# Feed-forward weights of a two-layer trunk split in units of four blocks, and a fourth seven-product step in every second column group

## The chip, the cores and the metric

The kernel runs on one core of one Trainium2 chip. The metric is the device time of one execution, in microseconds. Beside the time there is a profile: one execution of the program taken by the hardware profiler, with each instruction's start, length and the event that released it.

## What is computed

The program is a trunk of two layers on 256 rows of width 2048, all in float32. Layer 0 mixes with sliding-window attention beside an mLSTM, layer 1 with forgetting attention. After either mixer comes a SwiGLU feed-forward part with hidden width 5632, and a last RMSNorm ends the trunk. The change touches the feed-forward part above all:

```python
def swiglu(xn, w_gate, w_up, w_down):
    return (jax.nn.silu(xn @ w_gate) * (xn @ w_up)) @ w_down
...
h = h + mix.astype(h.dtype)
h = h + swiglu(rms_norm(h, norm_ffn[layer]), w_gate[layer], w_up[layer], w_down[layer])
```

## The kernel before

**Three matmuls for one product.** A float32 operand is split into a rounded part `hi` and the rest `lo = x - hi`. A product is then the sum of three matmuls: left hi by right hi, left hi by right lo, left lo by right hi (`three`, L508 to L511; in the plain projections L212 to L214). Activations are split once. Every weight block of 128 rows by 512 columns is loaded from memory by a DMA on the queue of the sync engine SP (`load_raw`, L117), copied to `hi` on ScalarE (ACT) and subtracted to `lo` on VectorE (DVE) (`split_chunk`, L173 to L181). A load takes two blocks, one above the other (CK = 2): 128 partitions by 1024 elements, 512 KB. So the two lines L177 and L178 hold most of the ScalarE and VectorE work of the kernel.

**Column groups.** Gate and up have 11 groups of 512 columns per layer (`ffn`, L599). In one group `pair_group` (L516) walks over the 2048 rows of the weights as eight k pairs (256 rows each), with a list of steps such as

```python
ORDER = ((0, 0), (1, 1), (0, 2), (1, 3), (0, 4), (1, 5), (0, 6), (0, 7))
```

The second number is the k pair. A step with a leading 0 is a plain step: two row halves of the activations (t = 0, 1) by two k blocks by two matrices (gate and up, or two neighbouring column groups of down) are eight block products, 24 matmuls. A step with a leading 1 is a mixed step: seven block products give the same sums (Strassen's scheme in Winograd's form), so 21 matmuls, at the price of sums of blocks. On the side of the activations these sums are made once per pair (`sums_of`, L253, called where the pair's transposed activations come up) and kept in `sx` and `sd`. On the side of the weights VectorE makes four new blocks at every mixed step (L568 to L571), and the four are split again (`split_plain`, L338). Four of the seven products accumulate in banks of PSUM of their own (`prods`); after the last mixed step `combine` (L523 to L530) adds them up on VectorE into the tile `c`, and after the last plain step L619 adds the plain accumulators. SiLU (L621) and the product with up (L623) follow; the result is transposed by DMA (L646 to L648), joined and split a group later (`join`, L649).

The PSUM banks alternate: a group's plain accumulators sit in one pool of four banks, its `prods` in the other, and the next group has them the other way round (`bank`, L513). So a group's first plain products need the banks that `combine` of the group before has read out.

The eleven groups run in three parts (`PARTS`: 3, 4 and 4 groups). After a part follows its share of the down product, two runs of `pair_group` with 6 or 8 k pairs, of which 2 or 3 are mixed (`DOWN`).

**Buffers.** `hi` and `lo` of the weights come from a pool of six slots of two blocks (`wp`, L100), the raw blocks of plain steps from four slots of two (`wr`, L101), those of mixed steps from four slots of two in the layer's own pool (`RAWS`), and the four sums of a mixed step from two slots (`ht`, `lt`, L578). A slot is written again when the last reader of its old content is done; for `hi` and `lo` that is a matmul. In the mixers the same mixed step runs with other buffers (`halves` is given); there the change alters no amount of work.

**Order.** All instructions of an engine run in the order in which the program lists them. That list is made at build time by a planner that plays the program with its own costs; `run_due` (L188) and `issue_after` pin a few pieces of work to a step.

Of the kernel before, what the change touches and what calls it, by code (L numbers as in the profile page):

```python
# [17 lines left out]
P = 128  # L18
# [17 lines left out]
ORDER = ((0, 0), (1, 1), (0, 2), (1, 3), (0, 4), (1, 5), (0, 6), (0, 7))  # L36
# [15 lines left out]
RAWS = 4  # L52
# [20 lines left out]
def trunk(  # L73
# [26 lines left out]
    wp = ctx.enter_context(tc.tile_pool(name="wp", bufs=6))  # L100
    wr = ctx.enter_context(tc.tile_pool(name="wr", bufs=4))  # L101
# [15 lines left out]
    def load_raw(w, k0, c0, n, pool=wr, bufs=4, raws=None):  # L117
        if raws:
            raw = raws.pop(0)
            raws.append(raw)  # L120
        else:
            raw = pool.tile([P, CK, NB], F32, tag="raw", name="raw", bufs=bufs)
# [17 lines left out]
    first = wr.tile([P, CK, NB], F32, tag="raw", name="raw", bufs=4)  # L140
# [32 lines left out]
    def split_chunk(raw, n):  # L173
        hi = wp.tile([P, CK, NB], F32R, tag="hi", name="hi")
        lo = wp.tile([P, CK, NB], F32R, tag="lo", name="lo")
# [5 lines left out]
        return hi, lo  # L181

# [70 lines left out]
    def sums_of(pool, sh, sl, copies, full=None, tags=("tmp", "tmp"), bufs=None, box=None):  # L253
# [10 lines left out]
        nc.vector.tensor_tensor(out=s[:, 2, :], in0=full[:, 0, 0, :], in1=full[:, 0, 1, :], op=ALU.subtract)  # L264
# [62 lines left out]
    def scrap(fp, n):  # L327
# [3 lines left out]
        elif n == 3:  # L331
            halves = [fp.tile([P, 3, NB], F32, tag=f"sd{i}", name="box", bufs=1)[:, 0:CK, :] for i in range(2)]
        else:
            halves = [fp.tile([P, CK, NB], F32, tag="raw", name="box", bufs=RAWS) for _ in range(2)]
# [181 lines left out]
    def pair_group(fp, par, lhs, sums, mats, order, todo=(), halves=None, inner=None, raws=None):  # L516
# [6 lines left out]
        def combine(prods):  # L523
            c = fp.tile([P, 4, NB], F32, tag="c", name="c", bufs=1)
            nc.scalar.copy(c[:, 0, :], prods[0])
            nc.vector.tensor_tensor(out=c[:, 2, :], in0=prods[3], in1=c[:, 0, :], op=ALU.add)
# [5 lines left out]
        for pos, (kind, pair) in enumerate(order):  # L532
            k0 = 2 * pair
            if inner is not None and pos == len(order) - 1:
                c = combine(prods)
                inner()
            if not kind:
                last = pos == len(order) - 1
                walk = [(i, t) for i in range(CK) for t in range(NT)]
                if last:  # L540
                    walk.sort(key=lambda it: it[1])
                for m, (w, c0) in enumerate(mats):
                    hi, lo = load_chunk(w, k0, c0, NB)
                    run_due(todo, pos)
                    for i, t in walk:
# [3 lines left out]
                            plain[m][t], ah[:, ts], al[:, ts], hi[:, i, :], lo[:, i, :],  # L549
# [6 lines left out]
            ra, rb = (load_raw(w, k0, c0, NB, fp, W_RAWS if halves else RAWS, raws) for w, c0 in mats)  # L556
            hg, lg = split_chunk(ra, NB)
            run_due(todo, pos)
            t4 = ra if halves else fp.tile([P, 2, NB], F32, tag="t4", name="t4", bufs=1)
# [762 lines left out]
```

## Time and profile before

| | |
|---|---|
| runs | 2076.74, 2077.82, 2078.33 us; median 2077.82 us |
| span of the profiled execution | 2076.6 us (its own time is not listed beside it) |
| TensorE (PE) busy | 2066.4 us, 9473 matmuls |
| VectorE (DVE) busy | 1824.5 us, 2410 instructions |
| ScalarE (ACT) busy | 1374.7 us, 1736 instructions |
| read from memory | 408.68 MB |

A busy time is the sum of an engine's instruction spans with overlaps counted once. Matmul spans overlap each other, so the rate of TensorE is read from the distance of two starts, not from the length of one. In a view by stretches each row gives, for a stretch of the span, the busy time and number of instructions of each engine, the granted clock, the DMA share and GB/s. In a view in order of time a row gives start, length, engine, line, tiles and, in brackets, the idle time before it with what ended it.

### The profile page before, as it was taken

The numbers are of one execution on the slowest core, as the hardware profiler recorded it, in microseconds if no ns is written. First come the engines' busy times: TensorE is split into PE (matmuls) and PEld (weight loads), VectorE is DVE, ScalarE is ACT, GpSimd is POOL, SyncE is SP. The second block draws the span as 40 slices with busy tenths as digits, with TensorE's granted clock in tenths as the row PEclk, the third lists the DMA queues.
The fourth block names the chain that finished last, engine by engine and source line by source line (L and its number), as shares of the span: only waits on it lengthen the run. The fifth ranks groups of instructions, "written<-read, shape, count | busy, mean of one in ns | idle before, by whom it ended". The sixth has DMA issues, their size and how long they took to land.

```text
span 2076.6 us, 26994 instructions
## 1 busy us (share of the span) xinstructions
PE 2066.4 (100%) x9473; PEld 1715.0 (83%) x9473; DVE 1824.5 (88%) x2410; ACT 1374.7 (66%) x1736; POOL 41.7 (2%) x66
## 2 busy tenths in 40 slices
PE   9999999999999999999999999999999999999998
PEld 7878888888888888888888888888888888888887
DVE  6788769999999999999899778689999999999994
ACT  6777678765676656667676776687655667456763
POOL 1010000000000000000000001000000000000000
PEclk9999999999999999999999999999999999999999
DMA  8566577666566666666576866586665667666764
GB/s 292 172 213 188 190 247 236 203 217 206 189 230 223 205 210 205 220 212 204 185 215 204 235 193 184 156 283 220 206 205 200 213 206 234 203 202 213 220 197 138
DMA packets 309575, 434.87 MB, mean 209 GB/s; under 512 B 106412, under 2 KB 114624, under 8 KB 309312
## 3 DMA queue, kind: packets, MB, share of 16 engines
q1 hardware_dynamic: 307088, 426.27, 65.1%
q0 software_dynamic: 1632, 5.80, 0.8%
q8 instruction: 74, 1.21, 0.2%
q10 hardware_dynamic: 720, 1.09, 0.2%
q14 instruction: 61, 0.50, 0.1%
HBM read 408.68 MB, written 2.12 MB: 198 GB/s over the span
## 4 chain that ended last, share of the span: by engine, by line
PE 97%; DVE 1%; ACT 1%; DMA 1%; issue 1%; SPq 0%; POOLq 0%; POOL 0%; ACTq 0%; DVEq 0%
PE acc L510 21%; PE acc L509 21%; PE acc L511 21%; PE acc L213 5%; PE acc L212 5%; PE acc L214 5%; PE prod L509 5%; PE prod L510 5%; PE prod L511 5%; PE p L369 1%; PE po L470 1%; DMA raw<-in_w_in_odd_dram 0%; ACT s L403 0%; PE po L471 0%; DVE lo L178 0%
## 5 line engine op out<-in xcount | busy, mean ns | idle before, releaser
L177 ACT CAST hi<-raw 128x1024 fp32r<-128x1024 f32 (+3 forms) x656 | 664.8, 1028 | 440.2 <-PE acc L511 269.1
L178 DVE TENSOR_TENSOR lo<-raw,hi 128x1024 fp32r<-128x1024 f32 (+3 forms) x656 | 772.8, 1192 | 146.3 <-ACT hi L177 143.5
L510 PE MATMUL acc<-lo,xh 128*128 128x512 f32 x1254 | 488.6, 390 | 0.0
L509 PE MATMUL acc<-hi,xh 128*128 128x512 f32 x1254 | 485.9, 390 | 0.5 <-ACT hi L177 0.5
L511 PE MATMUL acc<-hi,xl 128*128 128x512 f32 x1254 | 484.8, 389 | 0.0
L510 PEld LDWEIGHTS acc<-lo,xh 128*128 128x128 f32 x1254 | 235.4, 188 | 49.4 <-DVE lo L178 0.6
L509 PEld LDWEIGHTS acc<-hi,xh 128*128 128x128 f32 x1254 | 235.2, 188 | 49.5 <-ACT hi L177 0.7
L511 PEld LDWEIGHTS acc<-hi,xl 128*128 128x128 f32 x1254 | 235.4, 188 | 48.8
L510 PE MATMUL acc<-lo,mh 128*128 128x512 f32 x437 | 169.7, 389 | 0.0
L511 PE MATMUL acc<-hi,ml 128*128 128x512 f32 x437 | 168.4, 389 | 0.0
L509 PE MATMUL acc<-hi,mh 128*128 128x512 f32 x437 | 167.9, 389 | 0.0
L339 ACT CAST hi<-raw 128x512 fp32r<-128x512 f32 x109 | 67.6, 620 | 89.4 <-PE acc L511 80.5
L213 PE MATMUL acc<-lo,mh 128*128 128x512 f32 (+1 forms) x322 | 126.3, 392 | 0.0
L212 PE MATMUL acc<-hi,mh 128*128 128x512 f32 (+1 forms) x322 | 125.8, 391 | 0.0
L214 PE MATMUL acc<-hi,ml 128*128 128x512 f32 (+1 forms) x322 | 123.7, 391 | 0.0
L340 DVE TENSOR_TENSOR lt<-t,ht 128x1024 fp32r<-128x1024 f32 x95 | 115.8, 1219 | 5.2 <-ACT ht L339 5.1
L339 ACT CAST ht<-t 128x1024 fp32r<-128x1024 f32 x95 | 99.9, 1051 | 30.7 <-PE prod L511 28.8
L339 ACT CAST ht<-raw 128x1024 fp32r<-128x1024 f32 x95 | 99.7, 1050 | 29.7 <-PE acc L511 15.0
L340 DVE TENSOR_TENSOR lt<-raw,ht 128x1024 fp32r<-128x1024 f32 x95 | 115.7, 1218 | 1.8 <-ACT ht L339 1.8
L213 PE MATMUL acc<-lo,xh 128*128 128x512 f32 (+3 forms) x288 | 99.8, 348 | 0.2 <-DVE lo L178 0.2
L214 PE MATMUL acc<-hi,xl 128*128 128x512 f32 (+3 forms) x288 | 98.1, 344 | 0.0
L212 PE MATMUL acc<-hi,xh 128*128 128x512 f32 (+3 forms) x288 | 95.9, 347 | 0.3
(363 smaller groups left out, 3448.0 us busy)
## 6 DMA issues: line engine op xcount, KB each, us to landing
raw<-in_w_gate_dram SPq DMA_DIRECT2D x176, 512.0 KB, 4.5
raw<-in_w_up_dram SPq DMA_DIRECT2D x176, 512.0 KB, 4.6
raw<-in_w_down_dram SPq DMA_DIRECT2D x176, 512.0 KB, 5.1
raw<-in_w_in_odd_dram SPq DMA_DIRECT2D x88, 512.0 KB, 4.9
raw<-in_w_in_even_dram SPq DMA_DIRECT2D x51, 512.0 KB, 5.0
raw<-in_w_out_even_dram SPq DMA_DIRECT2D x32, 512.0 KB, 5.1
raw<-in_w_out_odd_dram SPq DMA_DIRECT2D x32, 512.0 KB, 4.8
hr<-in_w_in_even_dram SPq DMA_DIRECT2D x12, 512.0 KB, 4.6
```

The lines of the kernel that those rows point to most:

```text
L177: latest[0] = nc.scalar.copy(hi[:, k, 0:n], raw[:, k, 0:n])
L178: nc.vector.tensor_tensor(out=lo[:, k, 0:n], in0=raw[:, k, 0:n], in1=hi[:, k, 0:n].bitcast(F32), op=ALU.subtract)
L212: nc.tensor.matmul(o, ah[:, ts], hi, start=(k == 0), stop=False)
L213: nc.tensor.matmul(o, ah[:, ts], lo, start=False, stop=False)
L214: nc.tensor.matmul(o, al[:, ts], hi, start=False, stop=(k == k_all - 1 and cs.stop == n))
L339: nc.scalar.copy(dst_h, src)
L340: nc.vector.tensor_tensor(out=dst_l, in0=src, in1=dst_h.bitcast(F32), op=ALU.subtract)
L369: nc.tensor.matmul(pq[j % 2][:, j // 2, :], q_of(j, b), k_of(j)[:, 0:cols], start=True, stop=True)
L470: nc.tensor.matmul(po, v_of(j, 0), tt[:, j, 0:2, :].rearrange("p c q -> p (c q)"), start=True, stop=False)
L509: nc.tensor.matmul(o, ah, hi, start=start, stop=False)
L510: nc.tensor.matmul(o, ah, lo, start=False, stop=False)
L511: nc.tensor.matmul(o, al, hi, start=False, stop=stop)
```

## The change

It regroups the feed-forward part's weight work and adds ten mixed steps.

- **Units of four blocks.** `hi`, `lo` and raw become fixed tiles of four blocks used in turn: three pairs of `hi` and `lo` in all the kernel and a fourth in `close_layer`, two raw tiles for plain steps and two for mixed ones. Outside the feed-forward part a half of such a tile is handed out, in place of a slot of two blocks. A plain step of the feed-forward part still has two loads of 512 KB; then come two copies on ScalarE and one subtraction of 128x2048 on VectorE (before: two of 128x1024).
- **A mixed step** loads one matrix's two blocks in one DMA and the other's two in one DMA each, in reverse order. Three blocks are split by one copy and one subtraction of 128x1536. The four sums take three instructions: one of 128x1024 with a broadcast operand, and two of 128x512. They are split by two copies of 128x1024 and one subtraction of 128x2048. Signs of one block are turned for this (`sums_of` too), and the products are issued in another order.
- **combine** takes three additions in the feed-forward part (before: four); the last has 128x1024 with a broadcast operand.
- **The fourth mixed pair.** `ORDER` now has k pair 6 mixed too, at the step behind the mixed pair 5; it is used for odd groups, and the old list, now `LIGHT`, for even ones. The activations' sums of pair 6 are made for it, once a layer.

```diff
-ORDER = ((0, 0), (1, 1), (0, 2), (1, 3), (0, 4), (1, 5), (0, 6), (0, 7))
+ORDER = ((0, 0), (1, 1), (0, 2), (1, 3), (0, 4), (1, 5), (1, 6), (0, 7))
+LIGHT = ((0, 0), (1, 1), (0, 2), (1, 3), (0, 4), (1, 5), (0, 6), (0, 7))
...
-RAWS = 4
+RAWS = 2
...
-    wp = ctx.enter_context(tc.tile_pool(name="wp", bufs=6))
-    wr = ctx.enter_context(tc.tile_pool(name="wr", bufs=4))
+    wp = ctx.enter_context(tc.tile_pool(name="wp", bufs=1))
+    weights = [[wp.tile([P, 4, NB], F32R, name=f"{a}{i}") for a in ("hi", "lo")] for i in range(3)]
+    wr = ctx.enter_context(tc.tile_pool(name="wr", bufs=1))
+    raws_ = [[wr.tile([P, 4, NB], F32, name=f"raw{i}")] for i in range(2)]
+    spare = {}
+
+    def slot(ring):
+        spare.pop(id(ring), None)
+        ring.append(ring.pop(0))
+        return ring[-1]
+
+    def half_slot(ring):
+        kept = spare.pop(id(ring), None)
+        if kept:
+            return [t_[:, CK:, :] for t_ in kept]
+        kept = slot(ring)
+        spare[id(ring)] = kept
+        return [t_[:, 0:CK, :] for t_ in kept]
...
+    def split_wide(hi, lo, src, parts):
+        for ks in parts:
+            latest[0] = nc.scalar.copy(hi[:, ks, :], src[:, ks, :])
+        nc.vector.tensor_tensor(out=lo, in0=src, in1=hi.bitcast(F32), op=ALU.subtract)
...
+            if halves is None:
+                nc.vector.tensor_tensor(out=c[:, 1, :], in0=prods[3], in1=c[:, 0, :], op=ALU.add)
+                nc.vector.tensor_tensor(out=c[:, 2, :], in0=prods[2], in1=c[:, 1, :], op=ALU.add)
+                nc.vector.tensor_tensor(
+                    out=c[:, 1:4:2, :],
+                    in0=prods[1].rearrange("p (a n) -> p a n", a=1).broadcast_to([P, 2, NB]),
+                    in1=c[:, 1:3, :],
+                    op=ALU.add,
+                )
+                return c
...
+                if halves is None:
+                    (raw,) = slot(raws_)
+                    for m, (w, c0) in enumerate(mats):
+                        load_rows(raw[:, CK * m : CK * (m + 1), :], w, k0, c0)
+                    hi, lo = slot(weights)
+                    split_wide(hi, lo, raw, (slice(0, CK), slice(CK, 4)))
+                    run_due(todo, pos)
...
+            if halves is None:
+                raw = fp.tile([P, 4, NB], F32, tag="raw", name="raw", bufs=RAWS)
+                (wa, ca), (wb, cb) = mats
+                load_rows(raw[:, 0:CK, :], wa, k0, ca)
+                for k in range(CK):
+                    load_rows(raw[:, 3 - k : 4 - k, :], wb, k0 + k, cb)
+                hi, lo = slot(weights)
+                split_wide(hi[:, 0:3, :], lo[:, 0:3, :], raw[:, 0:3, :], (slice(0, 3),))
+                run_due(todo, pos)
+                nc.vector.tensor_tensor(
+                    out=raw[:, 0:4:3, :],
+                    in0=raw[:, 3:4, :].broadcast_to([P, 2, NB]),
+                    in1=raw[:, 0:3:2, :],
+                    op=ALU.subtract,
+                )
+                nc.vector.tensor_tensor(out=raw[:, 2, :], in0=raw[:, 2, :], in1=raw[:, 0, :], op=ALU.subtract)
+                nc.vector.tensor_tensor(out=raw[:, 1, :], in0=raw[:, 1, :], in1=raw[:, 2, :], op=ALU.subtract)
+                ht_, lt_ = slot(weights)
+                split_wide(ht_, lt_, raw, (slice(0, CK), slice(CK, 4)))
...
             three(prods[1], sh[:, 0, :], sl[:, 0, :], ht[0], lt[0], first, last)
+            three(plain[0][1], xb[:, t1], lb[:, t1], ht[3], lt[3], False, False)
+            three(prods[3], sh[:, 1, :], sl[:, 1, :], ht[2], lt[2], first, last)
             three(prods[2], sh[:, 2, :], sl[:, 2, :], ht[1], lt[1], first, last)
-            three(prods[3], sh[:, 1, :], sl[:, 1, :], ht[2], lt[2], first, last)
-            three(plain[0][1], xb[:, t1], lb[:, t1], ht[3], lt[3], False, False)
...
-                    fp, par, x_of, sums_x, [(w_gate[layer], g * NB), (w_up[layer], g * NB)], ORDER, todo
+                    fp, par, x_of, sums_x, [(w_gate[layer], g * NB), (w_up[layer], g * NB)], ORDER if g % 2 else LIGHT, todo
...
+            fourth = [fp.tile([P, 4, NB], F32R, name=f"{a}3", bufs=1) for a in ("hi", "lo")]
+            weights.append(fourth)
```

107 lines of the change are left out of this document (60 added, 47 removed).

## The prediction

> **What bounds the kernel now.** I read first the page's busy times and its chain of work, then the list of waits, then the view by stretches over one column group, and last the order of time within it.
>
> ```profile
> PE 2066.4 (100%) x9473; PEld 1715.0 (83%) x9473; DVE 1824.5 (88%) x2410; ACT 1374.7 (66%) x1736; POOL 41.7 (2%) x66
> ...
> PE 97%; DVE 1%; ACT 1%; DMA 1%; issue 1%; SPq 0%; POOLq 0%; POOL 0%; ACTq 0%; DVEq 0%
> ```
> ```profile
> PE acc L509 <- ACT hi L177: 0.5, 1, 0.5
> ...
> DVE lo L178 <- ACT hi L177: 143.5, 166, 5.5
> ...
> ACT hi L177 <- PE acc L511: 269.3, 187, 5.0
> ACT hi L339 <- PE acc L511: 80.8, 68, 1.9
> ```
>
> The chain that ended last is TensorE for 97%. In the whole feed-forward part TensorE waited once, 0.5 us. The waits run the other way: ScalarE stood 269.3 us in front of L177 until a matmul gave a weight slot back, and VectorE then 143.5 us for ScalarE. So the split runs ahead until its slots are full, and TensorE sets the pace. How close VectorE is behind shows only by stage; these are one gate and up group and one pair of down runs:
>
> ```profile
> core 0: us, PE busy (x) PEld busy (x) DVE busy (x) ACT busy (x) POOL busy (x), PEclk, DMA share, GB/s
> ...
> 620.82:662.30 41.48, 41.48 (x185) 34.35 (x184) 39.73 (x51) 28.47 (x33) 0.00 (x0) 1.00 0.66 216
> ...
> 703.78:786.74 82.96, 82.96 (x368) 68.69 (x367) 77.84 (x93) 43.76 (x48) 0.00 (x0) 1.00 0.66 211
> ```
> ```profile
> 650.95 0.39 PE L509 MATMUL prod<-hi,xh 128*128 128x512 f32 x1
> ...
> 652.99 0.39 PE L509 MATMUL prod<-ht,sx 128*128 128x512 f32 x1
> ```
> ```profile
> 620.82 0.58 ACT L525 COPY c<-prod 128x512 f32<-128x512 f32 x1
> ...
> 662.30 0.58 ACT L525 COPY c<-prod 128x512 f32<-128x512 f32 x1
> ```
>
> The stretch 620.82 to 662.30 is one period: from a group's `combine` copy (L525) to that of the next group. Between the two matmuls lie nine starts in 2.04 us, so a matmul costs 0.2267 us, whatever its span of 0.39 says. A group has five plain steps of 24 and three mixed ones of 21: 183 matmuls by 0.2267 are 41.49 us. The period is 41.48. TensorE has no gap at all, and VectorE is busy for 39.73 of it: 1.75 us of air, 4%. In the down runs the air is 5.12 in 82.96. ScalarE has 13 us of air and is no bound.
>
> **The change part by part. Matmuls.** Each odd group turns a plain step into a mixed one, 24 matmuls into 21. Odd are g = 1, 3, 5, 7, 9, in two layers: 10 groups by 3 matmuls by 0.2267 us are 6.80 us off TensorE, on the path that sets the end. An odd group's period falls from 41.48 to 40.80. Nothing else in the change takes a matmul away or adds one.
>
> The Trainium skill (TensorE: Matmul & The Clock Gate, section Back-to-back issue gap) gives N/2.4 + 2.5 ns for a warm matmul by itself, 216 ns here. By that the 30 matmuls would be 6.5 us; the distance in the rows above is longer, and the row decides.
>
> **VectorE, instruction by instruction.** The price is the distance of two starts, not the length:
>
> ```profile
> 578.47 0.69 DVE L569 TENSOR_TENSOR t<-raw 128x512 f32<-128x512 f32 x1
> 579.07 1.22 DVE L340 TENSOR_TENSOR lt<-raw,ht 128x1024 fp32r<-128x1024 f32 x1
> 580.21 0.68 DVE L340 TENSOR_TENSOR sd<-s,sd 128x512 fp32r<-128x512 f32 x1
> 580.81 4.63 DVE L178 TENSOR_TENSOR lo<-raw,hi 128x1024 fp32r<-128x1024 f32 x4
> ...
> 586.49 0.68 DVE L526 TENSOR_TENSOR c<-prod,c 128x512 f32<-128x512 f32 x1
> 587.21 0.69 DVE L527 TENSOR_TENSOR c<-prod,c 128x512 f32<-128x512 f32 x1
> ```
>
> A 128x512 subtraction gives way after 0.60 us (578.47 to 579.07), one of 128x1024 after 1.137 (four take 4.63, the last one 1.22 of it). So 512 elements cost 0.537 and every instruction 0.063 on top. That gives estimates for the two sizes that are new: 1.674 for 128x1536, 2.211 for 128x2048. L527, which reads what L526 wrote, starts after 0.72: a directly dependent instruction costs 0.12 more unless another fits between.
>
> A plain step: two of 1.137 become 2.211, a saving of 0.063. A mixed step: three of 1.137 and five of 0.60, 6.41, become 1.674 + 1.137 + two of 0.60 + 2.211 = 6.22, a saving of 0.19. `combine`: four of 0.60 become two and one of 1.137, a saving of 0.063. An even group (5 plain, 3 mixed) saves 0.95 and needs 38.78 of its 41.48 us. An odd group has one plain step less and one mixed more, 4.01: 42.79 against TensorE's 40.80. **Odd groups are 1.99 short, even ones 2.70 over.** An even and an odd one together: VectorE 81.57, TensorE 82.28.
>
> That strided and broadcast operands run at the plain rate, no row shows. From below, a second reading of the same block could cost nothing, a gain of 0.54 for each; from above, it could cost as much again as the instruction itself, 1.07: with four mixed steps and a `combine`, 5.4 us for an odd group, which would lead to the third rival's times. I take the plain rate, by the nearest row: `c<-prod,c` reads PSUM at 0.68, as the others read SBUF.
>
> The Trainium skill (VectorE: DVE Perf Modes, section The TRN2 errata) prices a float32 tensor_tensor by itself at (N+151)/0.96 ns, 157 ns fixed per instruction. By that an even group's 15 saved instructions would be 2.4 us and not 0.95, which favours the change. The spacing here shows that back to back most of that is hidden, 0.063 being left.
>
> **What carries the shortage.** The weights stand in four slots of four blocks; a plain step takes one, a mixed step two. While TensorE works on an even group's last plain step, three slots can hold the next group's first plain and mixed step: 2.21 + 6.22 = 8.4 us of VectorE work ahead, against 1.99 that are missing. Within an odd group the tight place is the mixed pairs 5 and 6, one behind the other: TensorE takes 42 by 0.2267, 9.52 us, VectorE needs 12.44. Before pair 5 starts, its two slots and the first slot of pair 6 can be full, so pair 6 lacks only its last split of 2.21, which waits for the plain step 4's slot. That is free with all of pair 5 to come. I cost this at nothing; if the cover is gone, it is the first rival.
>
> **ScalarE, DMA, buffers.**
>
> ```profile
> 587.23 1.06 ACT L177 CAST hi<-raw 128x1024 fp32r<-128x1024 f32 x1 [4.16 <-PE acc L511]
> ...
> 621.30 2.00 ACT L177 CAST hi<-raw 128x1024 fp32r<-128x1024 f32 x2
> ```
> ```profile
> raw<-in_w_gate_dram SPq DMA_DIRECT2D x176, 512.0 KB, 4.5
> ...
> raw<-in_w_in_even_dram SPq DMA_DIRECT2D x10, 256.0 KB, 2.9
> ```
>
> A plain step's subtraction now waits for two copies, 2.00 us where it was 1.06, and is itself 1.07 longer: the first matmul can start 2.0 us later after a slot falls free. The ring covers this, since a plain step's slot falls free a step or more before its matmuls are due (5.44 us for a plain step, 4.76 for a mixed one). A mixed step issues three DMAs on SP where there were two; two of 256 KB in a row land after some 5.8 us at worst against 4.5, and the two raw tiles of a kind are used in turn, while steps of a kind mostly come 10.2 us apart (5.44 + 4.76), so a load has about that long. Nothing.
>
> **The sums of pair 6 and the layer's start.** They fall into the first group of a layer, where VectorE is tightest:
>
> ```profile
> 330.00:400.00 70.00, 70.00 (x311) 57.96 (x310) 68.79 (x91) 54.88 (x65) 0.69 (x1) 1.00 0.76 241
> 400.00:441.50 41.50, 41.50 (x185) 34.37 (x184) 39.68 (x51) 28.37 (x31) 0.00 (x0) 1.00 0.66 205
> ...
> 1388.00:1458.00 70.00, 70.00 (x310) 57.98 (x309) 67.50 (x89) 53.01 (x64) 0.00 (x0) 1.00 0.71 231
> 1458.00:1499.50 41.50, 41.50 (x185) 34.35 (x183) 39.63 (x50) 28.40 (x32) 0.00 (x0) 1.00 0.66 208
> ```
> ```profile
> 338.43 0.28 DVE L264 TENSOR_TENSOR s<-full 128x128 f32<-128x128 f32 x1
> 338.63 0.28 DVE L262 TENSOR_TENSOR s<-full 128x128 f32<-128x128 f32 x1
> ...
> 401.27 1.23 DVE L178 TENSOR_TENSOR lo<-raw,hi 128x1024 fp32r<-128x1024 f32 x1 [1.22 <-ACT hi L177]
> ```
>
> Four sums at 0.20 and a split of 0.60 are 1.4 us; less the 0.95 saved, group 0 has 0.45 more. Group 1 has 42.79 - 39.73 = 3.06 more and 0.68 less time: together 4.19. VectorE's air to the end of group 1 is 1.82 in layer 0 (41.50 - 39.68; ahead of 401.27 there is next to none), and in layer 1 4.37 (2.50 + 1.87). So layer 0 lacks 2.4 us unless VectorE enters ahead, layer 1 nothing. The lead at 335 us is not in the rows: between 0 and 2.4 us of stall I take about half, 1.3.
>
> **Sum.** -6.80 + 1.3 = -5.5 us. On the profiled execution: 2076.6 to 2071.1. The median of the runs is 1.2 us above that span, so **2072.3 us**, 0.27% less. The part's two ends: 2071.0 without any stall, 2073.4 with all of it.
>
> **The rivals.** *First, slower: the lead is not carried over.* A lead can be kept only as far as slots are free, and the 269.3 us of ScalarE waiting say that they mostly are not. If a split of the odd group always finds its slot late, VectorE sets that group's pace: 42.79 us, or 43.39 with five more dependent pairs of 0.12 exposed, against 41.48 before. Ten groups: +13.1 to +19.1, **2091 to 2097**. The even groups can't give it back, since TensorE sets theirs. It decides from a lead of 1.99 us downward. For it: the units are twice as coarse and the order is fixed. Against it: 8.4 us of possible lead.
>
> The Trainium skill (Perfetto Trace Analysis, section Identifying the Most-Contended Engine) says to judge TensorE not by matmul busy time but by weight loading, and the others by occupancy. By that rule VectorE (39.73 of 41.48) stands ahead of TensorE (34.35 of weight loading), and this rival would come true in full. The equal spacing of the matmuls speaks against it here.
>
> *Second, half of it.* A quarter to a half of an odd group's shortage (1.99 + 0.6) is exposed, 0.65 to 1.29 us: 10 by that, less 6.80, gives -0.3 to +6.1, **2077.5 to 2083.9**, and down to 2074 for an eighth.
>
> *Third, coarse units starve TensorE in every group.* If the 2.0 us of later first matmul show once in each of the 22 groups, +44 - 6.8: **2115**.
>
> *Fourth, the change doesn't do what it says:* its matmul count must fall by 30; if spacing rises instead, the time stays at 2078. The spacing held through all of the groups, so I give it nothing of its own.
>
> **How the numbers follow.** Forecast (2070.5 to 2073.6) 0.48; still faster, as VectorE's savings close gaps elsewhere, 0.03; second rival 0.22, of which 0.18 lies within 0.2% and 0.04 above; first rival 0.21; third 0.06. A difference of 0.2%, 4.2 us, is about what a measurement of this kernel can tell from none. So faster 0.51, same 0.18, slower 0.31. The range runs from 2070 to 2094: 0.02 is left out below, half of the first rival and the third above.
>
> **What would show it.** Right: 9443 matmuls; an odd group's period of 40.8 us and an even one's of 41.5 between the L525 copies; TensorE's waits for VectorE below 3 us in total; VectorE's 128x2048 subtractions at 2.29 us long, 128x1536 at 1.76. Wrong: TensorE waits for a split's `lo` at the mixed pairs 5 and 6 or in the next group's first mixed step, again and again; VectorE without any idle time through odd groups; broadcast sums longer than 1.22 us.

## The result, and the profile after

| | before | after |
|---|---|---|
| median of 4 runs each | 2078.07 us | 2216.17 us (2212.99 to 2216.98) |
| ratio, 95% interval | | 1.0663 [1.0648, 1.0678] |
| span of the profiled execution | 2076.6 us | 2215.1 us |

138 us slower; 2072.3 was forecast, with a range that ended at 2094. The page's engine row and chain of work, after:

```profile
PE 2119.0 (96%) x9443; PEld 1709.0 (77%) x9443; DVE 1842.3 (83%) x1981; ACT 1371.5 (62%) x1657; POOL 43.2 (2%) x66
...
PE 34%; DVE 21%; DMA 9%; ACT 9%; issue 9%; SPq 2%; DVEq 0%; ACTq 0%; POOLq 0%; POOL 0%
```

The 30 matmuls are gone, and TensorE no longer carries the end: its share of the chain fell from 97% to 34%. VectorE, ScalarE and the DMAs now take turns in it. The list of waits says how (engine and line that waited, what for: us, times, longest):

```profile
DVE lo L211 <- ACT hi L210: 146.1, 104, 4.3
ACT hi L210 <- PE acc L542: 141.5, 82, 4.8
...
ACT hi L210 <- DMA raw<-in_w_up_dram: 112.2, 52, 6.7
ACT hi L210 <- DVE raw L622: 84.7, 27, 5.5
...
ACT hi L210 <- DVE raw L623: 49.3, 27, 5.7
...
ACT hi L210 <- DMA raw<-in_w_down_dram: 45.3, 29, 6.2
...
PE prod L540 <- ACT hi L210: 27.7, 46, 2.8
```

Before, ScalarE waited in the feed-forward parts mainly for free slots (for loads of gate and up 6.1 and 4.1 us); now it also waits 157.5 us for weights on their way (112.2 and 45.3) and 134.0 us for the sums that VectorE makes in the raw tiles (L622, L623), and TensorE waits for ScalarE. The period of one gate and up group, between two copies of `combine`, was 41.48 us. Three of them now:

```profile
core 0: us, PE busy (x) PEld busy (x) DVE busy (x) ACT busy (x) POOL busy (x), PEclk, DMA share, GB/s
573.94:624.98 51.04, 49.60 (x214) 39.48 (x213) 45.69 (x39) 31.30 (x32) 0.00 (x0) 1.00 0.71 235
624.98:670.72 45.74, 41.18 (x175) 32.06 (x174) 40.56 (x37) 29.21 (x30) 0.00 (x0) 0.99 0.56 178
670.72:717.54 46.82, 45.95 (x188) 36.53 (x188) 40.52 (x38) 27.87 (x29) 0.00 (x0) 0.94 0.64 209
```

The three stretches are 143.60 us long for 577 matmuls, which at 0.2267 us take 130.8: 12.8 us are gaps. VectorE now idles 5 to 6 us in a stretch and ScalarE 16 or more, so no engine is full. How that can be shows in one place, first by windows of 5 us, then in the chain of work in order of time (start, length, what), then on ScalarE and VectorE:

```profile
380.00:385.00 5.00, 5.00 (x24) 4.14 (x23) 5.00 (x5) 2.42 (x4) 0.00 (x0) 1.00 0.01 5
400.00:405.00 5.00, 5.00 (x24) 4.14 (x23) 1.35 (x2) 1.48 (x1) 0.00 (x0) 1.00 1.00 347
...
410.00:415.00 5.00, 2.92 (x11) 1.53 (x9) 5.00 (x8) 4.97 (x6) 0.00 (x0) 1.00 0.00 0
415.00:420.00 5.00, 3.98 (x10) 2.16 (x10) 5.00 (x6) 3.94 (x5) 0.00 (x0) 0.70 0.17 28
```
```profile
395.69 2.17 DVE lo L211
397.86 0.49 SPq L204
...
400.38 7.34 DMA raw<-in_w_up_dram
...
407.82 1.49 ACT hi L210
409.31 0.02 issue
409.33 0.04 DVE lo L211
```
```profile
396.93 2.00 ACT L210 CAST hi<-raw 128x1024 fp32r<-128x1024 f32 x2 [1.71 <-PE acc L542]
403.39 1.48 ACT L210 CAST hi<-raw 128x1536 fp32r<-128x1536 f32 x1 [4.46 <-DMA raw<-in_w_up_dram]
407.82 1.48 ACT L210 CAST hi<-raw 128x1536 fp32r<-128x1536 f32 x1 [2.95 <-DMA raw<-in_w_up_dram]
```
```profile
398.96 2.29 DVE L211 TENSOR_TENSOR lo<-raw,hi 128x2048 fp32r<-128x2048 f32 x1 [1.11 <-ACT hi L210]
404.90 1.76 DVE L211 TENSOR_TENSOR lo<-raw,hi 128x1536 fp32r<-128x1536 f32 x1 [3.65 <-ACT hi L210]
406.70 1.23 DVE L616 TENSOR_TENSOR raw<-raw 128x1024 f32<-128x1024 f32 x1
409.33 1.76 DVE L211 TENSOR_TENSOR lo<-raw,hi 128x1536 fp32r<-128x1536 f32 x1 [1.41 <-ACT hi L210]
```

From 380 to 385 hardly a byte moves (DMA share 0.01). The chain shows what a load waits for: a raw tile is free only when VectorE has ended the large subtraction that reads it (395.69), then SP issues several loads in a row (397.86 on). They come all at once and fill all DMA engines (share 1.00), and one of them takes 7.34 us. ScalarE waits for it, 4.46 and 2.95 us, VectorE for ScalarE, 3.65 us, and from 410 to 415 TensorE has run dry: 2.92 us busy of 5, while the DMAs stand still once more. Here the work passes in lumps from one engine to the next. Over the whole kernel SP waited 208 times for a large subtraction to free a raw tile, 798.2 us or 3.8 us each time; before it waited 407 times for one of two blocks (L178, mixers included), 1.8 us each time. The loads of one block each, which the prediction priced at 2.9 us, took longer (list of DMA issues, after: size in KB and median us from issue to landing):

```profile
raw<-in_w_up_dram SPq DMA_DIRECT2D x152, 256.0 KB, 4.4
raw<-in_w_down_dram SPq DMA_DIRECT2D x58, 256.0 KB, 5.6
```

**Where the time is.** For each kernel I added up, from the order of time on TensorE, by how much the distance of two starts exceeds 0.2267 us (0.11 for a small matmul), in the mixers with the output projections, and in the two feed-forward parts. Where a layer is cut is a choice: another cut moves up to 6 us from one column to the other, and the sums of the rows change by 2 us at most.

| kernel | us | gaps, mixers | gaps, feed-forward |
|---|---|---|---|
| before | 2077.8 | 30.1 | 0.9 |
| after | 2216.2 | 52.7 | 119.6 |
| after, three mixed pairs | 2192.6 | 53.5 | 88.6 |
| after, fine plain steps | 2216.7 | 54.6 | 117.0 |
| after, fine mixed steps | 2200.6 | 53.9 | 101.7 |
| after, all fine | 2180.7 | 53.5 | 84.9 |
| after, late fourth tile | 2197.6 | 33.8 | 119.6 |
| all fine, from pools | 2180.6 | 27.8 | 108.4 |
| units of four, from pools | 2259.6 | 50.1 | 164.8 |
| before + fourth pair | 2115.2 | 27.5 | 44.5 |
| before + fixed turns | 2092.1 | 31.9 | 12.0 |
| before + sums in place | 2096.8 | 27.4 | 19.5 |
| before + units of four in plain steps | 2110.4 | 44.7 | 14.4 |

After against before: 141 us more of gaps (22.6 in the mixers, 118.7 in the feed-forward parts), less 6.8 of matmuls, makes 134 of the 138 us.

### The profile page after: what moved, and what is told of

Same layout as the page of the kernel before. It is cut to its first block, busy times and chain, and to the rows that moved or that the text cites. A ratio compares the mean times of both kernels' runs of the same rounds, so it can differ in the third digit from the quotient of the medians.

```text
span 2215.1 us, 26290 instructions
## 1 busy us (share of the span) xinstructions
PE 2119.0 (96%) x9443; PEld 1709.0 (77%) x9443; DVE 1842.3 (83%) x1981; ACT 1371.5 (62%) x1657; POOL 43.2 (2%) x66
## 4 chain that ended last, share of the span: by engine, by line
PE 34%; DVE 21%; DMA 9%; ACT 9%; issue 9%; SPq 2%; DVEq 0%; ACTq 0%; POOLq 0%; POOL 0%
DVE lo L211 11%; PE acc L541 8%; PE acc L542 8%; PE acc L540 8%; ACT hi L210 5%; DMA raw<-in_w_up_dram 5%; DVE raw L616 2%; PE prod L541 2%; PE prod L542 2%; PE prod L540 2%; DMA raw<-in_w_down_dram 2%; DMA raw<-in_w_out_odd_dram 1%; DVE raw L622 1%; DVE raw L623 1%; PE acc L243 1%
## 5 line engine op out<-in xcount | busy, mean ns | idle before, releaser
L210 ACT CAST hi<-raw 128x1024 fp32r<-128x1024 f32 (+1 forms) x617 | 668.6, 1121 | 504.4 <-PE acc L542 141.5
L211 DVE TENSOR_TENSOR lo<-raw,hi 128x2048 fp32r<-128x2048 f32 (+1 forms) x361 | 762.9, 2132 | 146.5 <-ACT hi L210 146.1
L197 DVE TENSOR_TENSOR lo<-raw,hi 128x1024 fp32r<-128x1024 f32 (+3 forms) x239 | 270.3, 1144 | 116.7 <-ACT hi L196 115.5
L196 ACT CAST hi<-raw 128x1024 fp32r<-128x1024 f32 (+3 forms) x239 | 231.0, 985 | 135.6 <-PE acc L542 31.0
L542 PE MATMUL acc<-hi,ml 128*128 128x512 f32 x466 | 181.0, 389 | 0.0
L616 DVE TENSOR_TENSOR raw<-raw 128x1024 f32<-128x1024 f32 x105 | 128.1, 1220 | 0.9
L541 PEld LDWEIGHTS acc<-lo,mh 128*128 128x128 f32 x466 | 87.4, 188 | 27.2 <-DVE lo L211 8.8
L540 PEld LDWEIGHTS acc<-hi,mh 128*128 128x128 f32 x466 | 87.2, 188 | 21.1 <-ACT hi L210 3.4
L542 PEld LDWEIGHTS acc<-hi,ml 128*128 128x128 f32 x466 | 87.5, 188 | 18.0
L540 PE MATMUL prod<-hi,sx 128*128 128x512 f32 x228 | 81.1, 414 | 18.9 <-ACT hi L210 18.9
```

The costliest lines, as they stand in the source:

```text
L196: latest[0] = nc.scalar.copy(hi[:, k, 0:n], raw[:, k, 0:n])
L197: nc.vector.tensor_tensor(out=lo[:, k, 0:n], in0=raw[:, k, 0:n], in1=hi[:, k, 0:n].bitcast(F32), op=ALU.subtract)
L210: latest[0] = nc.scalar.copy(hi[:, ks, :], src[:, ks, :])
L211: nc.vector.tensor_tensor(out=lo, in0=src, in1=hi.bitcast(F32), op=ALU.subtract)
L540: nc.tensor.matmul(o, ah, hi, start=start, stop=False)
L541: nc.tensor.matmul(o, ah, lo, start=False, stop=False)
```

## The experiments

"One look" is a single run; the others have an interval. Runs of one kernel with gaps lay up to 9 us apart (2175.57 to 2184.17 us with all units fine). Pair 6's own sums of the activations are left out where an expectation says that it reads pair 5's; such a kernel doesn't compute the trunk and serves for its time alone. Several times lie in no range that was written down before: fine mixed steps, all fine, units of four from pools, fixed turns, sums in place, own tile, and a sum on GpSimd beside the fourth pair.

One thing goes along with every edit: the planner makes a new list. By the traces, ScalarE's order, which the edit itself leaves alone, departs from that of the kernel before within its first 500 instructions of some 1740, in the runs with fixed turns, with sums in place, with three additions, with the order of products and with a sum on GpSimd alike. No run holds the order fixed. The last three stayed at 2077 to 2078 us with another order, which speaks against a large share for the order and doesn't exclude one.

### Parts taken out of the changed kernel

Three mixed pairs everywhere, units kept (one look: 2192.6 us):
```diff
-ORDER = ((0, 0), (1, 1), (0, 2), (1, 3), (0, 4), (1, 5), (1, 6), (0, 7))
+ORDER = ((0, 0), (1, 1), (0, 2), (1, 3), (0, 4), (1, 5), (0, 6), (0, 7))
...
-                    fp, par, x_of, sums_x, [(w_gate[layer], g * NB), (w_up[layer], g * NB)], ORDER if g % 2 else LIGHT, todo
+                    fp, par, x_of, sums_x, [(w_gate[layer], g * NB), (w_up[layer], g * NB)], LIGHT, todo
```


> The changed kernel with three mixed pairs in every group (the fourth is undone), units of four blocks kept. Theory U (units: slots, raw tiles and subtractions come in lumps of four blocks, so the split of a unit starts late and TensorE runs dry in every group): 30 matmuls more, 6.8 us, and less VectorE work; it stays at 2180 to 2220 us. Theory V (overload: the fourth mixed step makes VectorE the bound in odd groups and nothing pays it back): it returns to 2075 to 2085 us.

The fourth pair's removal gives back 24 us. The rest of the loss is there without it, with VectorE busy for 1798.8 us, less than the 1824.5 of before: a shortage of VectorE alone doesn't explain it.

Plain steps fine again, by loads, copies and subtractions of two blocks (one look: 2216.7):
```diff
-                    (raw,) = slot(raws_)
...
-                    split_wide(hi, lo, raw, (slice(0, CK), slice(CK, 4)))
+                for m, (w, c0) in enumerate(mats):
+                    hm, lm = load_chunk(w, k0, c0, NB)
```


> The changed kernel with its plain steps as before (loads, slots, copies and subtractions of two blocks), mixed steps still in units of four, fourth pair kept. Theory U: a share of the gaps goes; plain steps are 5 of 8 steps and wait for loads of two blocks instead of four: 2110 to 2170 us. Theory V: VectorE does 0.06 us more per plain step, so 2216 or a little above.

Nothing regained. Mixed steps fine, plain ones coarse (one look: 2200.6):
```diff
-                split_wide(hi[:, 0:3, :], lo[:, 0:3, :], raw[:, 0:3, :], (slice(0, 3),))
...
+                    split_plain(hs, ls, src)
```


> The changed kernel with its mixed steps in pieces of two blocks (two loads, three splits of one or two blocks, four separate sums in place, each in its own half slot), plain steps still in units of four, fourth pair kept. Theory U: the long chain of a mixed step gets short again, 2100 to 2170 us; whichever of this and the run with fine plain steps is lower names the kind of step that does more harm. Theory V: 0.2 us more of VectorE per mixed step, 2216 to 2240 us.

16 us regained. Both fine, with the fourth pair and the fixed tiles kept (2180.7 us, ratio 1.049 [1.047, 1.0509]):

> The changed kernel with plain and mixed steps in pieces of two blocks, the fourth mixed pair of odd groups kept, and the combine of three additions kept. Theory U: the gaps go and the 30 matmuls remain saved, 2069 to 2085 us. Theory V: VectorE has even more to do, 2200 us or more.

The units are worth 35 us, not the 131 or more that theory U had. So 103 us lie in what is left: fourth pair, fixed turns, fourth tile, sums in place, combination, order of the products. Where the fourth tile joins the turns, it was moved from the start of `close_layer` to behind the output projection (one look: 2197.6):
```diff
         with tc.tile_pool(name=f"fp{layer}", bufs=2) as fp:
             fourth = ...
-            weights.append(fourth)
...
             todo = out_proj(w_out, idx, key, (*sx, fp))
+            weights.append(fourth)
```


> The changed kernel with the fourth weight tile taken into the turn after the output projection instead of before it. In the changed kernel's trace TensorE stands 7 us at the end of each mixer, waiting for the mixer's last results. Theory L (the fourth tile lies where the mixer's late tiles were, so its first use holds ScalarE's queue): about 15 us less, 2196 to 2204 us. Rival: no change, 2214 to 2218 us.

18.5 us regained, and by the table all of it in the mixers' column (52.7 to 33.8), none in the feed-forward parts.

### Pools in place of fixed tiles

All fine, slots from pools as before (one look: 2180.6), then units of four, slots from pools (one look: 2259.6); the edit of the first:
```diff
-    weights = [[wp.tile([P, 4, NB], F32R, name=f"{a}{i}") for a in ("hi", "lo")] for i in range(3)]
...
+    wp = ctx.enter_context(tc.tile_pool(name="wp", bufs=6))
```


> The kernel of e4 (everything in pieces of two blocks, fourth mixed pair, combine of three additions, sums in place) with slots taken from pools as before: six slots of weights, four of raw blocks, two of their own for the split sums. e4 took 2181 us. Theory F (fixed turns: a tile is bound to its place in the turn when the program is written, so the planner can no longer give the next free slot to whichever step is ready, and the splits of sums stand in one turn with everything else): 2068 to 2085 us. Theory V (overload by the fourth mixed step) or I (sums made in place in the raw tile, a longer chain): stays above 2140 us.

> The changed kernel with its units of four blocks, but the units taken from pools: three slots for the weights, two for raw blocks, and one slot of its own for the split sums. Theory F: most of the 138 us comes back, 2075 to 2110 us. Theory U (units of four as such): stays at 2180 to 2220 us.

The first moved the loss and didn't lessen it: mixers 53.5 to 27.8, feed-forward 84.9 to 108.4. With pools the plain and the mixed steps' split blocks have slots of their own and can't lend each other any; that this is the reason is argued, not shown. The second has one slot of four blocks for the split sums of a mixed step (before: two slots of two), and ScalarE waited 196.7 us for matmuls to free it (`ht`).

### Parts put alone on the kernel before

The fourth pair (2115.2 us, ratio 1.0187 [1.017, 1.0204]):
```diff
+HEAVY = ((0, 0), (1, 1), (0, 2), (1, 3), (0, 4), (1, 5), (1, 6), (0, 7))
...
-                    fp, par, x_of, sums_x, [(w_gate[layer], g * NB), (w_up[layer], g * NB)], ORDER, todo
+                    fp, par, x_of, sums_x, [(w_gate[layer], g * NB), (w_up[layer], g * NB)], HEAVY if g % 2 else ORDER, todo
```


> The kernel before with the fourth mixed pair in odd groups and nothing else of the change. Pair 6 reads the activations' sums of pair 5, so that they fit; its own sums, 1.4 us once a layer, are left out. Theory V: VectorE is short by 3 us per odd group, 2100 us or more. Theory F or U: 2069 to 2085 us.

37 us worse, in fine units and pools. The fixed tiles in turn (one look: 2092.1) and the four sums made in the raw blocks (one look: 2096.8):
```diff
-        hi = wp.tile([P, CK, NB], F32R, tag="hi", name="hi")
-        lo = wp.tile([P, CK, NB], F32R, tag="lo", name="lo")
+        hi, lo = half_slot(weights)
```


> The kernel before with one part of the change alone: weights and plain raw blocks stand in fixed tiles of four blocks whose halves are handed out in turn (six halves of weights, four of raw blocks), in place of pools of six and four slots; every instruction and load stays. Theory F: 2120 us or more. Theories U, V and I: 2078 us, since no unit, sum or step is changed.


```diff
-                else (t4[:, 0, :], t4[:, 1, :], ra[:, 0, :], ra[:, 1, :])
...
+            ta, tb, tc_, td = ra[:, 0, :], rb[:, 0, :], rb[:, 1, :], ra[:, 1, :]
```


> The kernel before with one part alone: a mixed step makes its four sums in the two raw blocks that it read, in place of two of them in a tile of their own. No instruction more or less, three mixed pairs. Theory I (the sums must wait until the copies and subtractions of the loaded blocks have read them, and both raw tiles stay taken until the sums are split, so the chain of a mixed step is longer and its next load later): 2115 to 2150 us. Rivals (the combine of three additions or the new order of products does the rest of the harm): 2078 us.

14 and 19 us, although neither adds an element to any engine's work. In place, both raw tiles of a step stay taken until the last split; before, one of them came free at L570. SP's waits for a free raw tile show who frees it, before and with the sums in place (lines of SP's list, each with what freed the tile):

```profile
SPq L123 <- DVE lo L178: 733.8, 407, 13.2
SPq L123 <- DVE lt L340: 190.0, 86, 8.2
SPq L123 <- DVE raw L570: 150.8, 40, 7.6
```
```profile
SPq L123 <- DVE lo L178: 924.5, 406, 13.5
SPq L123 <- DVE lt L340: 260.3, 165, 8.1
```

Loads now wait 165 times for a split of the sums, where it was 86, and never for L570. But the time of these waits fell (340.8 us for L340 and L570 together before, 260.3 now); what grew are the waits for the ordinary subtraction L178, 733.8 to 924.5 us. So the list shows that the tiles are held longer, and not how the 19 us come of it.

Plain steps in units of four (2110.4 us, ratio 1.0158 [1.0129, 1.0188]):
```diff
+                    (raw,) = slot(raws_)
...
+                    split_wide(hi, lo, raw, (slice(0, CK), slice(CK, 4)))
...
-                    hi, lo = load_chunk(w, k0, c0, NB)
```


> The kernel before with its plain steps outside the mixers in units of four blocks (two loads, two casts, one subtraction of 128x2048, tiles from pools of three and two wide ones), mixed steps as before, three mixed pairs everywhere. Theory U (a unit twice as large passes through two engines in a row, so each of them idles while the other has it, and the slots come free half as often; no fourth pair is needed for that): 2090 to 2130 us, with ScalarE waiting for slots (TensorE's acc or VectorE's raw) and VectorE for ScalarE. Rival W (with VectorE's 1.7 us of slack in a group the coarse units cost nothing, and do so only beside the fourth pair): 2073 to 2080 us.

The time came out in theory U's range, 33 us more, although VectorE has less work (1807.4 us busy, before 1824.5). Its waits did not: VectorE waited 94.1 and 17.2 us for ScalarE, less than the 143.5 before. What grew are waits for loads. The groups by line, with VectorE's large subtraction and its first sum of a mixed step, the waits of ScalarE for a load, and what SP's loads of mixed steps waited for:

```profile
L209 DVE TENSOR_TENSOR lo<-raw,hi 128x2048 fp32r<-128x2048 f32 x161 | 367.5, 2283 | 24.1 <-ACT hi L208 17.2 <-PE acc L537 6.5 <-PE prod L539 0.3
...
L605 DVE TENSOR_TENSOR t<-raw 128x512 f32<-128x512 f32 x95 | 65.0, 685 | 50.6 <-DMA raw<-in_w_up_dram 42.8 <-DMA raw<-in_w_down_dram 7.8
```
```profile
ACT hi L367 <- DMA raw<-in_w_up_dram: 67.2, 18, 6.3
```
```profile
SPq L141 <- DVE raw L607: 313.0, 55, 10.3
```

The subtraction has its forecast length; what is new is that the mixed step behind it waits for its weights: 50.6 us of idle time before the first sum, where it was 1.3 (L568). Its load goes out later, since SP waits 313.0 us for the third sum (L607) to free a raw block, where it was 150.8 (L570). By the table half of the loss is in the mixers, where by the code a slot of four blocks is handed out in halves and comes free only when both are read; that this makes the loss there is not shown.

The combination in three additions (2077.6 us, ratio 1.0001 [0.9991, 1.0012]) and the order of the products (2077.4 us, ratio 1.0001 [0.999, 1.0011]):
```diff
+                nc.vector.tensor_tensor(
+                    out=c[:, 1:4:2, :], in0=prods[1].rearrange(...).broadcast_to([P, 2, NB]), in1=c[:, 1:3, :], op=ALU.add,
+                )
```


> The kernel before with the change's combination of the products in three additions and its order of the quarters, and nothing else. Theory S (VectorE has about 1.7 us of 41.5 to spare in a group, and only what adds to its work or to the path of a step costs): the combination is 0.06 us shorter, so 2076 to 2079 us. Rival C (the last addition of 1.2 us holds all quarters back until it ends, so the accumulators of the next group come free later, 0.6 us at each of 33 combinations): 2085 to 2100 us.


```diff
+            three(plain[0][1], xb[:, t1], lb[:, t1], ht[3], lt[3], False, False)
...
-            three(plain[0][1], xb[:, t1], lb[:, t1], ht[3], lt[3], False, False)
```


> The kernel before with the change's order of the products, in which the plain product with the fourth weight sum comes second instead of last, and nothing else. The second pair of sums is needed three matmuls (0.68 us) earlier. Theory S: TensorE has steps in store, so 2076 to 2080 us. Rival R (it has none in store at the mixed steps, and waits 0.68 us in each of about 120): up to 80 us slower, and not under 2095 us.

Nothing either time.

### Is it VectorE that the fourth pair lacks?

The fourth pair alone, but with two of the four weight sums left out in odd groups' mixed steps (2074.4 us, ratio 0.9985 [0.9975, 0.9994]):
```diff
-            nc.vector.tensor_tensor(out=tc_, in0=rb[:, 1, :], in1=ta, op=ALU.subtract)
-            nc.vector.tensor_tensor(out=td, in0=ra[:, 1, :], in1=tc_, op=ALU.subtract)
+            if order is not HEAVY:
+                nc.vector.tensor_tensor(out=tc_, in0=rb[:, 1, :], in1=ta, op=ALU.subtract)
+                nc.vector.tensor_tensor(out=td, in0=ra[:, 1, :], in1=tc_, op=ALU.subtract)
```


> f3 (the kernel before with the fourth mixed pair in odd groups, 2115 us) with two of the four weight sums left out at every mixed step of an odd group, 4 by 1.2 us less of VectorE per odd group and nothing else. By the rows of before an odd group needs 43.9 us of VectorE against 40.8 of TensorE; without the two sums 39.1. Theory V (the loss of f3 is VectorE's shortage): 2069 to 2078 us. Rival W (two mixed steps in a row run out of slots or banks, whatever VectorE's time): 2100 to 2120 us.

All 37 us come back, and 3 of the 6.8 that the matmuls should give. Two groups (an even and an odd one) in the window view, first of the fourth pair alone, then without the two sums:

```profile
589.06:679.47 90.41, 87.92 (x376) 71.19 (x376) 84.54 (x108) 58.89 (x65) 0.00 (x0) 0.98 0.65 200
```
```profile
584.41:667.47 83.06, 83.06 (x368) 68.79 (x367) 77.33 (x97) 59.09 (x65) 0.00 (x0) 1.00 0.71 212
```

TensorE has no gap once VectorE has 77 us to do in 83. So two mixed steps in a row cost little by themselves (rival W fell), and in fine units the fourth pair's loss hangs on these two sums. They are work for VectorE, and they also lie on the path from a mixed step's load to its products, 1.2 us at each step; the run doesn't tell the two apart. A plain shortage it is not: with the fourth pair alone VectorE idles for 5.9 of the 90.41 us. The run leaves out work that the result needs, so it is no version to keep.

Could that work go elsewhere? One of the four sums on GpSimd, without the fourth pair (2078.4 us, ratio 1.0005 [0.9995, 1.0014]) and with it (2106.1 us, ratio 1.0138 [1.0121, 1.0155]):
```diff
-            nc.vector.tensor_tensor(out=tb, in0=rb[:, 1, :], in1=rb[:, 0, :], op=ALU.subtract)
+            eng = nc.vector if halves else nc.gpsimd
+            eng.tensor_tensor(out=tb, in0=rb[:, 1, :], in1=rb[:, 0, :], op=ALU.subtract)
```


> The kernel before with only that one weight sum moved to GpSimd, three mixed pairs everywhere. Theory V: TensorE already runs without gaps, so relief of VectorE buys nothing: 2074 to 2079 us. Rival P (the longer chain or a hold of VectorE): slower, 2085 to 2110 us, as the run with the sums in place (2096.8) was by its longer chain.

> The kernel before with the fourth mixed pair in the odd groups (as in the run with the fourth pair alone, 2115.2 us), and with one of the four weight sums, the one that waits for no other (second block less first block of up), made on GpSimd in every mixed step outside the mixers. Pair 6 reads pair 5's sums of the activations, as in that run. Theory V (VectorE's shortage is the loss): each mixed step is rid of about 0.6 us of VectorE, so an odd group needs 43.9 - 2.4 = 41.5 us against 40.8 of TensorE and an even one about 38 against 41.5: the loss of 37 us falls by 20 to 37 us, to 2078 to 2095 us; were it below 2073.5, it would beat both kernels. Rival P (GpSimd's sum is slower than VectorE's, its 128x512 rows of the kernel before are 1.44 us, and it lies in the chain before the split, or it holds VectorE up): no gain, 2110 to 2130 us, and VectorE waits for GpSimd at the split of the first two sums.

The first came out in theory V's interval, but for another reason: VectorE was not relieved. Its groups by line, then GpSimd's, three mixed pairs:

```profile
L568 DVE TENSOR_TENSOR t<-raw 128x512 f32<-128x512 f32 x95 | 114.3, 1203 | 0.0
L572 DVE TENSOR_TENSOR raw<-raw 128x512 f32<-128x512 f32 x109 | 84.5, 775 | 1.5
```
```profile
L570 POOL TENSOR_TENSOR t<-raw 128x512 f32<-128x512 f32 x95 | 197.9, 2084 | 1214.3 <-DVE lt L340 723.5 <-DVE raw L571 387.5 <-DMA raw<-in_w_out_odd_dram 63.3
```

The sum that VectorE makes at the same time takes 1203 ns where the kernel before has 684, and VectorE's busy time rose from 1824.5 to 1848.5 us with 95 instructions less. With the fourth pair, 9 of the 37 us came back, well short of theory V's 20. So no version that does all the work beats the kernel before.

The fourth pair with the change's combination and order, in fine units from pools, two sums in a tile of their own (one look: 2136.7), and the fourth pair with the order of products alone (2111.8 us, ratio 1.0165 [1.0135, 1.0194]):

> f1 (2181 us) with two of the four sums in a tile of their own again; pools of two blocks, fourth mixed pair, the combine of three additions and the new order of products stay. Pair 6 reads pair 5's activation sums, its own are left out, so that the tile fits. Theory I: close to the fourth pair alone (2115 us), 2100 to 2125 us. Rivals: above 2160 us.

> The kernel before with the fourth mixed pair in the odd groups (pair 6 reads pair 5's sums of the activations) and the change's order of the products, in which the second pair of sums is needed three matmuls (0.68 us) earlier. The order alone cost nothing on the kernel before, the fourth pair alone gave 2115.2. Theory R (where VectorE is short, TensorE runs up against each mixed step, and 0.68 us earlier is 0.68 us of waiting in some 30 of them): 2130 to 2140 us, which is the 21 us that the fourth pair lost beside the new combination and order. Rival C (the 21 us come from the combination in three additions): 2112 to 2119 us.

The first stands 44 us below the same kernel with all four sums in the raw blocks (2180.6), against 19 for them alone; it also leaves out pair 6's own sums, a few instructions per layer. The second frees the order of products; theory R fell (2111.8 is a hair below rival C's range). Some 21 us between 2115 and 2137 stay unexplained: the three additions are the largest edit left, and by themselves they cost nothing.

## Why the prediction was wrong, point by point

- **What bounds the kernel before** was read rightly, but 1.75 us of air on VectorE was taken for something to spend. The sums in place add no work and cost 19 us. The sum on GpSimd fills VectorE to 81.29 of two groups' 82.96 us and costs nothing:

```profile
579.34:662.30 82.96, 82.96 (x367) 68.69 (x367) 81.29 (x96) 56.96 (x63) 12.10 (x6) 1.00 0.73 216
```

  So VectorE's busy time alone doesn't decide. When slots and raw blocks come free is what the costly edits have in common; that this is the cause is argued, since the planner's order changed with them.
- **Matmuls, -6.80 us:** the count fell by 30 as forecast. The gain could show only with VectorE relieved, and then half of it.
- **VectorE's instructions:** the sizes were right, the broadcast at the plain rate as well (groups by line, VectorE, after):

```profile
L211 DVE TENSOR_TENSOR lo<-raw,hi 128x2048 fp32r<-128x2048 f32 x256 | 580.4, 2287 | 110.6 <-ACT hi L210 110.4
L211 DVE TENSOR_TENSOR lo<-raw,hi 128x1536 fp32r<-128x1536 f32 x105 | 184.1, 1753 | 35.9 <-ACT hi L210 35.7
L616 DVE TENSOR_TENSOR raw<-raw 128x1024 f32<-128x1024 f32 x105 | 128.1, 1220 | 0.9
```

  2.29 us was forecast and 2.287 measured, 1.76 and 1.753, 1.22 and 1.220. VectorE's work was not what was missed. Its waits for ScalarE grew with less work to do: 146.1 us in front of these subtractions and 116.5 in front of those of two blocks (L197), against 143.5 in front of L178 before.
- **"What carries the shortage … I cost this at nothing": failed.** The fourth pair alone, without any other part, lost 37 us. In the two groups of the windows above 90.4 us went by for 376 matmuls, which take 85.2, so 5.2 are gaps. That is more than the 2.4 us by which VectorE's work for an odd group (43.9 by the rows of before) exceeds 41.48; so the lead was not carried over, as the first rival said, and something beyond the shortage came on top. But 2091 to 2097 for all of the change was still far too low.
- **"ScalarE, DMA, buffers … Nothing": failed, and weighs most.** "The ring covers this" and "a load has about that long" are the sentences. Units of four in plain steps alone cost 33 us. The fixed turns (14) and the sums in place (19) stand in no term of the sum. Loads of 256 KB were priced by a row of 2.9 us, two in a row at 5.8 "at worst"; each took 4.4 and 5.6 us at the median (up and down), near that bound, and 7.34 in the place shown, past it. By the code each of the three edits leaves a step with larger tiles, with tiles held longer or with tiles taken in a fixed turn, and the list of waits of the changed kernel shows two ends of it: 157.5 us of ScalarE for loads, 134.0 for sums. The third rival came nearest, with 2.0 us per group; by the table the feed-forward parts lost 118.7 us in 22 groups, 5.4 each with their share of down.
- **The layer's start, 1.3 us:** the sums of pair 6 were not measured alone. What does cost time there was not on the list at all: a fourth tile that joins the turns before the output projection, 18.5 us.
- **The rivals' rule.** By the Trainium skill (Perfetto Trace Analysis, section Identifying the Most-Contended Engine) VectorE's occupancy would set the pace. The traces don't agree: with the fourth pair alone VectorE is busy for 84.54 of 90.41 us, in the changed kernel for 40.56 of 45.74, and TensorE's matmuls take 130.8 of the 143.60 us shown. No engine's occupancy explains the period.
- **The account.** Alone on the kernel before: 37 + 14 + 19 + 33 + 0 + 0, and 18.5 for the fourth tile (by moving it in the changed kernel), make 122 of 138 us. That is no proof of the sum, since the parts don't add: undoing the plain units alone regained nothing, undoing both kinds 35; the in-place sums cost 19 alone and 44 beside the fourth pair. Why the combination seems to cost something beside the fourth pair stays open. That the late tile holds up the turns until the mixer's last readers are done, I argue from the code; the run shows only where the time was.

## What to carry to other kernels

Here one engine ran without a gap and a second one was 96% full behind it, and each of three edits that hold buffers longer cost 14 to 33 us, without more work on any engine. So count for each tile from the load to its last reader, and not the busy times alone. Larger instructions save a fixed cost that back-to-back issue had mostly hidden (0.063 us each here), and pay with the time for which two engines wait for one another. Try such a change one part at a time.

## What the runs showed of the hardware

**After a dry stretch TensorE ran slowly for a while.** After the dry stretch from 410 to 415 us the granted clock of the next window is 0.70 (above); over the whole execution it is 0.989, and 0.999 in the kernel before. Order of time on TensorE in it:

```profile
418.65 0.63 PE L542 MATMUL acc<-hi,xl 128*128 128x512 f32 x1
419.08 0.63 PE L540 MATMUL acc<-hi,xh 128*128 128x512 f32 x1
419.50 0.63 PE L541 MATMUL acc<-lo,xh 128*128 128x512 f32 x1
419.93 0.60 PE L542 MATMUL acc<-hi,xl 128*128 128x512 f32 x1
```

The starts are 0.427 us apart, against 0.2267 before. The Trainium skill (TensorE: Matmul & The Clock Gate, section Wait — 56ns, not 53.3ns?) gives 512 columns at half clock as 426.7 ns, and the trace agrees. Added up over the changed kernel, distances of 0.40 to 0.45 us cost 13 us more than 0.2267 would, against 3 in the kernel before: some 10 of the 138 us are slow matmuls behind a wait.

**VectorE waits for GpSimd.** Order of time in the run with one sum on GpSimd and three mixed pairs, GpSimd, then VectorE:

```profile
576.60 2.21 POOL L570 TENSOR_TENSOR t<-raw 128x512 f32<-128x512 f32 x1 [9.49 <-DVE lt L340]
```
```profile
577.57 1.79 DVE L568 TENSOR_TENSOR t<-raw 128x512 f32<-128x512 f32 x1
579.28 1.21 DVE L340 TENSOR_TENSOR lt<-raw,ht 128x1024 fp32r<-128x1024 f32 x1
```

GpSimd ends at 578.81; VectorE's subtraction takes 1.79 us instead of 0.68 and ends 0.55 us after that. The Trainium skill (SBUF — State Buffer, section SBUF: two separate sides) calls the port that the two share an exclusive lock, held for a whole instruction, which also binds a VectorE operation with two operands in SBUF. That is what this row looks like.
